# A fourth raw weight buffer in the mixers of a two-layer hybrid decoder, paid for with single copies of the rotary step's small tiles

## Chip, core and metric

The kernel runs on one core of a Trainium2 chip. The metric is the device time of one launch in microseconds (us); lower is better. A core has five engines with queues of their own: TensorE (PE, with its weight loads shown as PEld), VectorE (DVE), ScalarE (ACT), GpSimd (POOL) and SyncE (SP), which here only issues DMAs.

## The reference

Two layers over 512 tokens of width 1024, all in float32. A layer is a mixer and an MLP:

```python
def hybrid_layer(x, ...):
    h = rmsnorm(x, norm_mix)
    z = h @ w_in                       # 1024 -> 4360 columns
    q_a, k_a, v_a, q_m, k_m, v_m, o_m, if_m, gates = jnp.split(z, splits, axis=-1)
    q_a = partial_rope(rmsnorm(q_a, att_q_norm), cos, sin)   # 8 heads of 64, first 16 dims turned
    k_a = partial_rope(rmsnorm(k_a, att_k_norm), cos, sin)   # 2 heads of 64
    att = sliding_window_attention(q_a, k_a, v_a, sinks)     # window 128, blocks of 128
    hm = mlstm_chunkwise(q_m, k_m, v_m, i_pre, f_pre)        # 4 heads, exact, running-max stabiliser
    hm = rmsnorm(hm, m_head_norm) * sigmoid(o_m)
    mixed = sigmoid(g_a) * (att @ w_att_branch) + sigmoid(g_m) * (hm @ w_m_branch)
    x = x + mixed @ w_out
    u = relu(rmsnorm(x, norm_ffn) @ w_ff1)                   # 1024 -> 4096
    return x + (u * u) @ w_ff2
```

## The kernel before

*Matrix products.* Each float32 operand is split into a rounded high part (`h`) and the rest (`l`), both of type float32r, and a product is three matmuls: high by high, high by low, low by high (`mm3`). For a weight chunk of 128 x 512 this is what happens in the mixer, in `chunk`: SP loads it into a tile of the pool `wraw` (L161 or L166); ACT copies it to `wh` (L186); DVE subtracts and gives `wl` (L187); both lie in the pool `wsp`, four buffers each. Then PE runs the chunk's matmuls: 4 slices of 128 by 3. A tile of `wraw` is free again when its `wl` is made, a pair of `wsp` when PE has read it.

*A mixer* runs, in this order, the projections q and k,v,i,f by tokens (`tok_steps`), mLSTM's q,k and the branch gates by features (`feat_steps`), the value and output-gate columns as seven products instead of eight (`vo_steps`; their loads are L813 and, with added halves, POOL's L817), the two attention projections (`a_steps`, from `w_att_branch`), the mLSTM projection (`m_step`, from `w_m_branch`, loads L1098 into `wraw` too, split by L196 and L197) and `w_out` (`p_step`, again seven products; loads L1111, L1120). `weave` lays between the steps of these products the side work: rope, attention (8 units of a block and a key head in each layer), the gates, the mLSTM.

*Order.* No order is written out by hand for whole engines. A planner goes through the instructions by priority and simulates the engines by a cost model; `tc.high_priority` pulls an instruction ahead, `tc.issue_after` puts it behind another on its engine. The planner also knows which buffer is free when, so the number of buffers of a pool enters into the order of every engine. DMAs of SP are issued in the order of SP's queue: one that waits for its buffer holds those behind it.

*Rope* (`rope`) scales the heads on DVE (L591) and then, on POOL, makes t1 = x cos (L594), t2 = the swapped halves times sin (L595, L597), and writes the sum back (L599). It runs for each of 4 blocks on the 2 key heads and the 8 query heads. t1 and t2 come from the pool `small`, tags `rp2`, `rq2` (128 bytes a partition) and `rp8`, `rq8` (512 bytes), three buffers each as all tags of that pool have.

*Room.* SBUF tiles of a partition, one after the other: constants, `small`, `inp` (the normed activations), and from there the phase's own pools. Mixer and MLP take turns in that last room (mixer 0, MLP 0, mixer 1, MLP 1), so a tile of one phase waits for the tiles of the phase before that lie under it (`reuse_waits="tile"`). In units of 2,048 bytes from the start of that room, worked out from the pools' sizes in their order:

| units before | mixer pool | units after the change |
|---|---|---|
| 0-3 | `wraw` | 0-4 |
| 3-11 | `wsp` (4 wh, 4 wl) | 4-12 |
| 11-34 | `act` (23 slots) | 12-35 |
| 34-42 | `prods` | 35-43 |
| 42-60 | `tmp` (18 slots) | 43-61 |
| from 60 | `mid`: `kvi`, `sel`, `cm2`, then `mid10`, `mid6` | from 61 |

| units, before and after | MLP pool |
|---|---|
| 0-14 | `uraw`: seven tiles of 4,096 bytes |
| 14-26 | `comb` |
| 26-34 | `uspl` (uh, ul) |
| 34-50 | `spl`: 4 wh (34-42), 4 wl (42-50), 128 x 1024 each |
| 50-60 | raw weights 9, 8, 7, 10, 3 |
| 60-64 | raw weights 0, 1 |
| 64-70 | raw weights 4, 5, 6 |
| 70-72 | raw weight 2 |

*The MLP* loads its raw weights (512 KB each) by SP at L1299 in the order 0, 1, 2, 9, 8, 7, 10, 3, 4, 5, 6, each issued behind the one before; adds further blocks to them by POOL (L1425, L1674); splits them by `two_parts` (L1263 on ACT, L1264 on DVE).

Of the kernel before, what the change touches and what calls it, by code (L numbers as in the profile page):

```python
# [16 lines left out]
P = 128  # L17
# [9 lines left out]
ROPE = 16  # L27
# [6 lines left out]
def hybrid_kernel(ctx, tc, x, norm_mix, w_in, att_q_norm, att_k_norm, att_sinks, m_gate_bias,  # L34
# [27 lines left out]
    def nm(s):  # L62
        uid[0] += 1
        return f"{s}_{uid[0]}"
# [4 lines left out]
    def pool(phase, name, bufs):  # L69
        now[name] = phase.enter_context(tc.tile_pool(name=name, bufs=bufs, reuse_waits="tile"))  # L70
        return now[name]
# [29 lines left out]
    def sm(shape, tag, bufs=None):  # L101
        return small.tile(list(shape), F32, tag=tag, name=nm(tag), bufs=bufs)
# [340 lines left out]
    def mixer(l, norm, late, order, phase):  # L443

        W = w_in[l]
        pool(phase, "wraw", 3)
        pool(phase, "wsp", 4)
        pool(phase, "act", 23)
        prods = pool(phase, "prods", 1)
# [137 lines left out]
        def rope(xv, b, nh):  # L587

            r0 = 0 if nh == HQ else 8
            ct, st = tabs[nh != HQ]  # L590
            ve.tensor_tensor(xv, xv, rqk[:, b, r0:r0 + nh].unsqueeze(2).to_broadcast([P, nh, HD]), op=ALU.mult)  # L591
            t1 = sm([P, nh, ROPE], f"rp{nh}")
            t2 = sm([P, nh, ROPE], f"rq{nh}")
            gp.tensor_tensor(t1, xv[:, :, 0:ROPE], ct[:, l, b:b + 1, :].to_broadcast([P, nh, ROPE]), op=ALU.mult)  # L594
            gp.tensor_tensor(t2[:, :, 0:8], xv[:, :, 8:16],  # L595
                             st[:, l, b:b + 1, 0:8].to_broadcast([P, nh, 8]), op=ALU.mult)
            gp.tensor_tensor(t2[:, :, 8:16], xv[:, :, 0:8],  # L597
                             st[:, l, b:b + 1, 8:16].to_broadcast([P, nh, 8]), op=ALU.mult)
            gp.tensor_tensor(xv[:, :, 0:ROPE], t1, t2, op=ALU.add)  # L599
# [9 lines left out]
        def k_vec(b):  # L609
            rope(kvi[:, b, 0:128].rearrange("p (h d) -> p h d", d=HD), b, HKV)  # L610
# [36 lines left out]
        def q_vec(b):  # L647
            rope(q_tok[b].rearrange("p (h d) -> p h d", d=HD), b, HQ)
# [1185 lines left out]
    for l in range(DEPTH):  # L1834
        with start if l == 0 else ExitStack() as phase:
            if l > 0:
                psum_pools(phase, 3)
            norm = mixer(l, norm, late, order, phase)
        with ExitStack() as phase:
            psum_pools(phase, 2)  # L1840
            norm = mlp(l, norm, phase)
        late = []
        if norm:
            late = [(0.5 + 0.5 * k, lambda k=k, norm=norm: turn_behind(norm, 6 + k)) for k in range(2)]
            late += [(1.25, lambda norm=norm: norm.squares(1))]
            late += norm.steps(0, 1.5, 0.5, lambda k, norm=norm: turn_behind(norm, k))
        order = [4, 5, 6, 7, 0, 1, 2, 3]
# [40 lines left out]
```

## Time and profile before

| | us |
|---|---|
| median of 3 runs (lowest, highest) | 1265.22 (1262.96, 1265.27) |
| the profiled execution | 1263.76 |
| its span, first to last instruction | 1262.1 |
| PE busy in it | 1255.6 |
| DVE busy | 1034.8 |
| ACT busy | 813.3 |
| POOL busy | 283.2 |

In the profile a line number is that of the kernel's source. PE's matmuls overlap in the records, since their ends are modelled, so a single one shows longer than the distance to the next. Names are the program's tiles with the buffer numbers left out, `out<-in`. The view of waits lists for each engine who ended its idle time; for SP, which only issues, it lists how long the queue stood. Times inside the profile are counted from the start of the span.

### The profile page before, as it was taken

The numbers are of one execution on the slowest core, as the hardware profiler recorded it, in microseconds if no ns is written. First come the engines' busy times: TensorE is split into PE (matmuls) and PEld (weight loads), VectorE is DVE, ScalarE is ACT, GpSimd is POOL, SyncE is SP. The second block draws the span as 40 slices with busy tenths as digits, with TensorE's granted clock in tenths as the row PEclk, the third lists the DMA queues.
The fourth block names the chain that finished last, engine by engine and source line by source line (L and its number), as shares of the span: only waits on it lengthen the run. The fifth ranks groups of instructions, "written<-read, shape, count | busy, mean of one in ns | idle before, by whom it ended". The sixth has DMA issues, their size and how long they took to land.

```text
span 1262.1 us, 19896 instructions
## 1 busy us (share of the span) xinstructions
PE 1255.6 (99%) x7170; PEld 1098.8 (87%) x7170; DVE 1034.8 (82%) x1645; ACT 813.3 (64%) x1442; POOL 283.2 (22%) x373
## 2 busy tenths in 40 slices
PE   9999999999999999999999999999999999999998
PEld 7888888888999899999888888888889999999987
DVE  5788988688998877878857989876889978778787
ACT  5578578645785665656554885876467766556563
POOL 4514131021122021031115042310303211311300
PEclk9999999999999999999999999999999999999999
DMA  5424573468899889997224354634779988998953
GB/s 159 114 69 134 127 130 93 142 137 212 179 250 182 233 170 211 235 187 190 36 75 118 89 137 110 117 111 132 156 208 189 240 191 228 171 223 207 201 134 100
DMA packets 145538, 199.68 MB, mean 158 GB/s; under 512 B 11032, under 2 KB 85632, under 8 KB 145440
## 3 DMA queue, kind: packets, MB, share of 16 engines
q0 software_dynamic: 50432, 68.30, 33.9%
q1 hardware_dynamic: 94016, 129.72, 33.5%
q8 instruction: 56, 0.92, 0.3%
q10 hardware_dynamic: 992, 0.40, 0.1%
q14 instruction: 42, 0.34, 0.1%
HBM read 195.24 MB, written 2.10 MB: 156 GB/s over the span
## 4 chain that ended last, share of the span: by engine, by line
PE 99%; DMA 0%; ACTq 0%; DVE 0%; issue 0%; DVEq 0%
PE mm L47 84%; PE aux L47 13%; PE aux L52 3%; DMA grow<-in_norm_mix_dram 0%; ACTq L373 0%; ACTq L380 0%; DVE x L1327 0%; DVEq L1884 0%
## 5 line engine op out<-in xcount | busy, mean ns | idle before, releaser
L1263 ACT ACTIVATE wh<-raw 128x1024 fp32r<-128x1024 f32 x224 | 235.0, 1055 | 149.9 <-PE mm L47 75.9
L1264 DVE TENSOR_TENSOR wl<-raw,wh 128x1024 fp32r<-128x1024 f32 x224 | 271.3, 1221 | 73.5 <-ACT wh L1263 70.7
L47 PE MATMUL mm<-i,wh 128*128 128x256 f32 (+1 forms) x1344 | 331.1, 339 | 0.0
L47 PEld LDWEIGHTS mm<-i,wh 128*128 128x128 f32 x1344 | 223.8, 190 | 19.4
L47 PE MATMUL mm<-i,wl 128*128 128x256 f32 (+1 forms) x672 | 224.7, 335 | 0.0
L47 PE MATMUL mm<-wh,uh 128*128 128x512 f32 x440 | 172.1, 391 | 0.0
L47 PE MATMUL mm<-wl,uh 128*128 128x512 f32 x440 | 171.7, 390 | 0.0
L47 PE MATMUL mm<-wh,ul 128*128 128x512 f32 x440 | 171.3, 389 | 0.0
L1425 POOL DMA_DIRECT2D raw<-in_w_ff_dram x56 | 72.5, 1375 | 349.3 <-DVE wl L1264 85.4
L47 PEld LDWEIGHTS mm<-i,wl 128*128 128x128 f32 x672 | 127.4, 190 | 13.5
L186 ACT ACTIVATE wh<-w 128x512 fp32r<-128x512 f32 (+1 forms) x143 | 85.3, 603 | 60.9 <-PE mm L47 44.0
L187 DVE TENSOR_TENSOR wl<-w,wh 128x512 fp32r<-128x512 f32 (+1 forms) x143 | 95.5, 671 | 34.8 <-ACT wh L186 34.0
L47 PE MATMUL mm<-t,wh 128*128 128x256 f32 x576 | 104.5, 283 | 0.0
L47 PE MATMUL mm<-wh,i 128*128 128x512 f32 (+1 forms) x352 | 99.5, 357 | 0.0
L47 PEld LDWEIGHTS mm<-wh,ul 128*128 128x128 f32 x440 | 82.6, 188 | 17.5
L47 PEld LDWEIGHTS mm<-wh,uh 128*128 128x128 f32 x440 | 82.8, 188 | 16.2
L47 PEld LDWEIGHTS mm<-wl,uh 128*128 128x128 f32 x440 | 82.8, 188 | 15.5
L47 PEld LDWEIGHTS mm<-t,wh 128*128 128x128 f32 x576 | 90.7, 192 | 1.3
L1674 POOL DMA_DIRECT2D raw<-in_w_ff_dram x40 | 48.4, 1214 | 169.8 <-DVE wl L1264 120.7
L47 PE MATMUL mm<-t,wl 128*128 128x256 f32 x288 | 81.5, 283 | 0.0
L1327 DVE SCALAR_TENSOR_TENSOR x<-mm,ms,x 128x512 f32<-128x512 f32 x102 | 72.4, 745 | 10.7 <-PE mm L47 10.4
L47 PEld LDWEIGHTS mm<-wh,i 128*128 128x128 f32 x352 | 62.0, 188 | 8.6
(336 smaller groups left out, 2536.6 us busy)
## 6 DMA issues: line engine op xcount, KB each, us to landing
raw<-in_w_ff_dram SPq DMA_DIRECT2D x144, 512.0 KB, 6.0
raw<-in_w_ff_dram POOLq DMA_DIRECT2D x96, 512.0 KB, 7.8
w<-in_w_in_dram SPq DMA_DIRECT2D x112, 256.0 KB, 2.8
a<-in_w_in_dram POOLq DMA_DIRECT2D x32, 256.0 KB, 5.7
qa<-in_w_out_dram POOLq DMA_DIRECT2D x12, 512.0 KB, 6.0
a<-in_w_in_dram SPq DMA_DIRECT2D x16, 256.0 KB, 4.4
w<-in_w_att_branch_dram SPq DMA_DIRECT2D x16, 256.0 KB, 3.1
w<-in_w_m_branch_dram SPq DMA_DIRECT2D x16, 256.0 KB, 2.7
```

The costliest lines, as they stand in the source:

```text
L47: latest[0] = nc.tensor.matmul(*args, **kw)
L52: latest[0] = nc.tensor.transpose(*args)
L186: sc.activation(wh[:, :off], raw[:, :off], AF.Copy)
L187: ve.tensor_tensor(wl[:, :off], raw[:, :off], f32(wh[:, :off]), op=ALU.subtract)
L1263: last_high[0] = sc.activation(hi, src, AF.Copy)
L1264: last_rest[0] = ve.tensor_tensor(lo, src, f32(hi), op=ALU.subtract)
L1327: ve.scalar_tensor_tensor(xh[:, cc], ps[i][:, cc], ms[j][:, b:b + 1], xh[:, cc], op0=ALU.mult, op1=ALU.add)
L1425: return gp.dma_start(to[h], src(h, i, j), accum_op=ALU.add)
L1674: gp.dma_start(to[h], src(h, i, j), accum_op=ALU.add)
```

## The change

The pool `wraw` gets four buffers in both mixers. The rope's t1 and t2 get one buffer for each tag instead of three. This frees 2 x 2 x (512 + 128) = 2,560 bytes a partition below the phase pools and takes 2,048 bytes more inside the mixers' room; the tables above show what that does to the places.

```diff
     def mixer(l, norm, late, order, phase):
 
         W = w_in[l]
-        pool(phase, "wraw", 3)
+        pool(phase, "wraw", 4)
         pool(phase, "wsp", 4)
         pool(phase, "act", 23)
...
             ve.tensor_tensor(xv, xv, rqk[:, b, r0:r0 + nh].unsqueeze(2).to_broadcast([P, nh, HD]), op=ALU.mult)
-            t1 = sm([P, nh, ROPE], f"rp{nh}")
-            t2 = sm([P, nh, ROPE], f"rq{nh}")
+            t1 = sm([P, nh, ROPE], f"rp{nh}", 1)
+            t2 = sm([P, nh, ROPE], f"rq{nh}", 1)
             gp.tensor_tensor(t1, xv[:, :, 0:ROPE], ct[:, l, b:b + 1, :].to_broadcast([P, nh, ROPE]), op=ALU.mult)
```

## The prediction

> **What bounds the kernel now.** I read the page first: busy shares, the chain that ended last, then the waits of TensorE.
>
> ```profile
> span 1262.1 us, 19896 instructions
> PE 1255.6 (99%) x7170; PEld 1098.8 (87%) x7170; DVE 1034.8 (82%) x1645; ACT 813.3 (64%) x1442; POOL 283.2 (22%) x373
> PE 99%; DMA 0%; ACTq 0%; DVE 0%; issue 0%; DVEq 0%
> ```
>
> PE works 1255.6 of 1262.1 us, and the chain back from the end is PE from one end to the other. So 6.5 us is all the time in which PE visibly does nothing. Next, the view of waits for PE alone, and the busy time by stretch (stretch, its length, then busy us and instruction count of PE, PEld, DVE, ACT, POOL, the granted clock, DMA share and GB/s). The first mixer ends at about 316, the second lies between about 628 and 942.
>
> ```profile
> PE aux L47 <- POOL ones L114: 1.2, 1, 1.2
> PE aux L52 <- DMA grow<-in_norm_mix_dram: 0.8, 1, 0.8
> 0.00:28.00 28.00, 25.96 (x124) 20.94 (x124) 12.77 (x22) 16.20 (x34) 15.25 (x37) 1.00 0.62 175
> 28.00:130.00 102.00, 101.85 (x545) 86.35 (x546) 86.69 (x213) 72.58 (x202) 36.92 (x70) 1.00 0.41 106
> 130.00:200.00 70.00, 70.00 (x333) 57.92 (x333) 65.74 (x134) 49.32 (x103) 18.94 (x26) 1.00 0.54 115
> 380.00:628.00 248.00, 248.00 (x1517) 223.52 (x1516) 202.25 (x199) 152.02 (x166) 47.83 (x41) 1.00 0.82 183
> 700.00:800.00 100.00, 99.89 (x494) 82.55 (x493) 91.74 (x202) 73.93 (x192) 26.15 (x41) 1.00 0.48 120
> 1005.00:1262.00 257.00, 252.87 (x1537) 227.22 (x1535) 205.58 (x204) 150.36 (x163) 45.46 (x37) 1.00 0.81 182
> ```
>
> The idle 6.5 us is placed: 2.04 at the start (two waits of 1.2 and 0.8, for a memset and for the gains), 4.13 behind the last matmul, and 0.15 + 0.11 = 0.26 in the two attention stretches. No wait of PE for a weight is listed at all. The clock is 1.00 throughout. Whatever helps the weights of the mixers can win 0.26 us of visible idle time.
>
> **The change part by part.**
>
> *The fourth raw buffer.* What it takes away are waits of SP for a buffer, and waits of ACT for a transfer. The waits of SP in 20 to 254 us, then in 640 to 880 (total, times, longest):
>
> ```profile
> SPq L166 <- DVE wl L187: 93.8, 36, 11.0
> SPq L166 <- DVE wl L187: 95.7, 41, 11.0
> ```
>
> The load of a chunk is issued as soon as the chunk three before it has been split (`wl`). With four it follows the chunk four before, so it is issued one chunk earlier. The waits of ACT, in 28 to 254 and then in 628 to 880:
>
> ```profile
> ACT wh L186 <- PE mm L47: 18.3, 15, 2.6
> ACT t L196 <- DMA w<-in_w_m_branch_dram: 3.5, 3, 1.8
> ACT wh L186 <- DMA w<-in_w_in_dram: 3.4, 4, 1.4
> ACT wh L186 <- DMA w<-in_w_att_branch_dram: 2.6, 3, 1.3
> ACT wh L186 <- PE mm L47: 25.8, 21, 2.6
> ACT t L196 <- DMA w<-in_w_m_branch_dram: 3.8, 3, 2.4
> ACT wh L186 <- DMA w<-in_w_in_dram: 3.8, 4, 1.7
> ACT wh L186 <- DMA w<-in_w_att_branch_dram: 2.2, 2, 1.3
> ```
>
> The transfers hold ACT for 3.5 + 3.4 + 2.6 = 9.5 us in the first mixer and 3.8 + 3.8 + 2.2 = 9.8 in the second; about 19 us of ACT's waiting can go. ACT then waits for the next thing, which the same rows show: a `wh` buffer that PE's matmuls free (18.3 and 25.8 us, four `wsp` buffers, unchanged). And nothing of it reaches PE. One chunk that waited for its transfer, the fourth of the second mixer:
>
> ```profile
> 629.72 2.19 SPq L166 DMA_DIRECT2D w<-in_w_in_dram  x3
> 632.29 0.63 ACT L186 ACTIVATE wh<-w 128x512 fp32r<-128x512 f32 x1 [0.84 <-DMA w<-in_w_in_dram]
> 632.96 0.69 DVE L187 TENSOR_TENSOR wl<-w,wh 128x512 fp32r<-128x512 f32 x1
> 644.04 0.48 PE L47 MATMUL mm<-wh,i 128*128 128x512 f32 x1
> ```
>
> Its `wl` is done at 632.96 + 0.69 = 633.65; PE gets to it at 644.04, after three chunks of 12 matmuls with the transposes of the norm between. So 10.4 us of cover lie over the 0.84 us that would go. Tighter is the first mixer around 40 us, where PE takes the 264-wide chunks faster; but the stretch 28 to 130 has 0.15 us of idle PE in all. Gain: between 0 and 0.26 us; I take 0.1.
>
> What it may cost. SP's queue is in order: a load issued earlier lets the loads behind it (L813, L1098, L1120) go earlier as well. In the first 28 us an earlier weight could take bandwidth from the x loads: 256 KB at the 175 GB/s of the first stretch is 1.5 us. But those loads stand ahead of it by `issue_after`, and after its two waits PE isn't idle there; I take 0, with 1.5 as the far end.
>
> *One copy of the rope's small tiles.* The instructions are the same; only the reuse distance shrinks. The rope's last POOL instruction on the q half (min/median/max ns):
>
> ```profile
> L599 POOL TENSOR_TENSOR a<-rp,rq x8: 453/482/791, 56.7 to 690.3; 128x128 f32<-128x128 f32 x8
> ```
>
> Both tiles are written (L594 to L597) and read (L599) by POOL alone, in its own order, and in POOL's timeline every L599 stands ahead of the next L594 of the same width already. So the single copy asks for no order that isn't there. Were it not so, a rope would wait for one L599, at most 0.79 us, on an engine that is 22% busy. I take 0; the far end is one such wait per layer that shows at PE, 2 x 0.79 = 1.6 us.
>
> *What lies over what.* 2 KB more for `wraw`, 2.5 KB less below it: seen from the mlp, whose pools use the same room, every mixer pool behind `wraw` moves up one 2 KB slot (units counted from the phase pools' start, in the tables of the section on the kernel). Waits for reused room change at the mixer's end. Two moves count.
>
> First, the mlp's raw 0 (units 60 to 62) lay over `kvi` and now lies over the last `tmp` slot and `kvi`. SP's issues at this place, SP's waits by what ended them, and a raw transfer's landing time:
>
> ```profile
> 276.17 35.24 SPq L1299 DMA_DIRECT2D raw<-in_w_ff_dram  x11
> SPq L1299 <- DMA x<-st: 34.5, 3, 17.5
> SPq L1299 <- DVE i L197: 16.9, 2, 8.6
> DMA to landing us min/median/max: 3.6/6.8/16.9
> ```
>
> Raw 0 is issued at 276.17; then SP stands 17.5 us for a stage tile (to 294) and 8.6 us for a split that reads a `tmp` tile (to 304). At the worst raw 0 also waits to 304, with raws 1 and 2 behind it, which land 6.8 us later, at 311 to 312. They are first read at:
>
> ```profile
> 313.36 1.04 ACT L1263 ACTIVATE wh<-raw 128x1024 fp32r<-128x1024 f32 x1
> 314.44 1.23 DVE L1264 TENSOR_TENSOR wl<-raw,wh 128x1024 fp32r<-128x1024 f32 x1 [2.17 <-ACT wh L1263]
> 310.37 0.48 PE L47 MATMUL mm<-wh,a 128*128 128x512 f32 x1
> 315.71 0.39 PE L47 MATMUL mm<-wh,a 128*128 128x512 f32 x1
> 316.62 0.49 PE L47 MATMUL mm<-i,wh 128*128 128x256 f32 x2
> 316.94 0.29 PE L47 MATMUL mm<-i,wl 128*128 128x256 f32 x1
> ```
>
> So 20 us of delay are hidden, with 1 to 2 us to spare in the worst case. Cost 0.
>
> Second, the first `wh` of the mlp (units 34 to 36) lay over `prods` and now has half of it over the last `act` slot. Four of those slots hold the operands of the mixer's last product, whose 24 matmuls PE runs from 310.37 to 315.71 + 0.39 = 316.1. The product goes by token halves of its operands, so two of the four come free halfway, at about 313.2, and two at 316.1; all others are free before. `wl` is ready at 314.44 + 1.23 = 315.67, and PE wants it at 316.94: 1.27 us of cover. If the slot is free before 313.36 + 1.27 = 314.6, nothing is lost; if only at 316.1, 316.1 - 314.6 = 1.5 us in each layer. Of 23 slots two are bad, and the planner can take another `wh` buffer first; I take 0, with 3 us as the far end.
>
> *Sum.* 1263.76 us of the profiled execution (1262.1 of span and 1.7 around it) - 0.1 = 1263.7. The three runs have their median 1.5 us above the profiled one, at 1265.22; so 1265.1 for a median.
>
> *A rule against the 99%.* The row above has PEld at 57.92 of 70 us (83%) in 130 to 200, and at 223.52 of 248 (90%) in the mlp. The Trainium skill, Perfetto Trace Analysis, section Identifying the Most-Contended Engine, says that the busy share of matmuls is a bad measure, since they are pipelined, and that the busy share of weight loads is a better one. By that rule the mixers have hidden gaps; by the busy row they have 0.26 us. The spacing of matmuls decides between them; pieces of the chain with start, us and count:
>
> ```profile
> 135.86 13.83 PE mm L47 x60
> 150.12 13.63 PE mm L47 x60
> 254.20 51.88 PE mm L47 x228
> ```
>
> 512-wide matmuls follow each other every 230.5, 227.2 and 227.5 ns. The lower share in the mixers comes from longer matmuls, not from gaps; at most 0.2 us in 13.83 is hidden.
>
> **The rivals.**
>
> *Faster, hidden gaps.* If those 0.2 us in 13.83 were late weights everywhere, the two mixers (630 us) would hide 9 us. For it: 230.5 against 227.2. Against it: no wait of PE in the list, and cover of 10 us over the chunk shown. Taken at a third: 1262. Chance 0.06.
>
> *Slower, the mlp's first `wh`.* The mechanism above: its room is free only when PE leaves the mixer's last product. It decides from 314.6 on, and costs up to 1.5 us twice: 1268. For it: 1.27 us of cover is the least that I found; against it, the planner's choice among four `wh` buffers. Chance 0.09.
>
> *Slower, another order.* The planner orders ACT and DVE by its own clock; with raw weights there earlier it can put one more split ahead of a link of the softmax or mLSTM chain. The low half of a split:
>
> ```profile
> L187 DVE TENSOR_TENSOR wl<-w,wh x143: 421/685/978, 7.7 to 875.7; 128x512 fp32r<-128x512 f32 x127, 128x264 fp32r<-128x264 f32 x16
> ```
>
> One split more ahead is 0.69 us on DVE, which is at 92% in 700 to 800; if each of the 16 attention units of both layers paid it to PE, 11 us; a third of them, 4 us: 1269. Chance 0.08.
>
> *The change does nothing*, since SP stands at other waits anyway: the same time as the forecast, and counted with it.
>
> **How the numbers follow.** The runs span 1262.96 to 1265.27, 2.3 us or 0.18%; 0.2% (2.5 us) is about what a measurement here can tell from no change. No change in time: 0.77, at 1265.1, own range 1263 to 1266.5. Faster rival 0.06, slower ones 0.17 at 1268 and 1269. Faster by over 0.2% needs less than 1262.7: 0.06. Slower needs more than 1267.7: about 0.15 of the slower cases' 0.17. Same: 0.79. The range reaches from the low end of the runs to 1268.5, where the first slower case is held and the second begins.
>
> **What would show it.** Right: SP's wait for `wl` L187 shorter, ACT's 19 us of waits for w transfers nearly gone and its waits for PE longer, PE idle 6.5 us as before, raw 0 of the mlp issued near 296 to 304 and not at 276. Wrong: a wait of PE listed in the mixers or at 316 and 942, PE's matmuls in the mixers further apart than 227 to 231 ns, or the second mixer's start or end moved against the first matmul by over 1 us.

## The result: 0.6% slower, and the profile after

| | before | changed |
|---|---|---|
| median of 6 runs each, us | 1263.49 | 1271.66 |
| lowest to highest, us | 1262.96 to 1265.27 | 1268.9 to 1273.08 |
| the profiled execution, us | 1263.76 | 1268.90 |
| its span, us | 1262.1 | 1267.2 |

The ratio of changed to before is 1.0058 (95% interval 1.0043 to 1.0072). A second set of runs gave 1.0050 (1.0038 to 1.0063). A ratio is estimated from all runs of both kernels and is not the quotient of the two medians. Two runs below, 5970.37 us in e_force and 1294.61 us in e_rope1, lie far above the others of their kernel and are counted in no ratio or median.

The mean of the six runs is 7.3 us above that before. The profiled execution is the fastest of the six, and its span is 5.1 us longer; these 5.1 us are what the views below account for. The other five left no trace; three of them, at 1272.23 to 1273.08, have a mean clock of 0.998 or 0.999.

The page of the changed kernel: its span, busy times and the chain that ended last.

```profile
span 1267.2 us, 19899 instructions
PE 1256.4 (99%) x7170; PEld 1098.9 (87%) x7170; DVE 1034.0 (82%) x1645; ACT 813.7 (64%) x1442; POOL 282.7 (22%) x373
PE 97%; DMA 1%; DVE 1%; ACT 1%; issue 0%; SPq 0%; ACTq 0%; DVEq 0%
```

The work is the same; the chain is no longer PE from end to end, and PE is idle for 1267.2 - 1256.4 = 10.8 us where it was 6.5. PE's waits in the changed kernel (total, times, longest):

```profile
PE mm L47 <- DVE wl L1264: 3.0, 2, 1.5
PE aux L47 <- POOL ones L114: 1.2, 1, 1.2
PE mm L47 <- ACT i L199: 0.8, 2, 0.4
PE aux L52 <- DMA grow<-in_norm_mix_dram: 0.6, 1, 0.6
PE mm L47 <- DVE i L200: 0.6, 2, 0.3
```

Three waits are new, each twice, that is once in each layer: 3.0 + 0.8 + 0.6 = 4.4 us. Two are the same as before, at the start of the kernel. The stretches say where the new ones are: 30 us around the start of the first mlp and 34 us around that of the second, before and then changed (columns as in the prediction).

```profile
310.00:340.00 30.00, 30.00 (x230) 28.71 (x229) 26.56 (x32) 23.84 (x36) 3.80 (x4) 1.00 0.80 209
936.00:970.00 34.00, 34.00 (x249) 32.10 (x248) 30.37 (x35) 26.33 (x39) 6.25 (x5) 1.00 0.78 191
```

```profile
310.00:340.00 30.00, 27.71 (x205) 25.87 (x204) 23.99 (x29) 21.74 (x34) 2.58 (x2) 1.00 0.68 176
936.00:970.00 34.00, 31.71 (x233) 29.54 (x232) 28.01 (x33) 24.58 (x38) 3.37 (x3) 1.00 0.71 188
```

PE loses 2.29 us in each. Counted by the starts of its matmuls, whose ends are only modelled, it is 3.0 us in each: the distance of each start from the one before, less the median distance for the width of that one, summed over 300 to 340 is 3.4 us against 0.4 before, and over 940 to 980 it is 3.3 against 0.3. That is 6.0 us in all, of which the start of the kernel gave back some 0.4 in this execution and the rest of the span some 0.5, in pieces below 0.3: 5.1 = 1267.2 - 1262.1.

Where PE waits, the timeline of the changed kernel's PE shows, rows with a wait in brackets:

```profile
316.32 0.60 PE L47 MATMUL mm<-i,wh 128*128 128x256 f32 x3
318.40 0.39 PE L47 MATMUL mm<-i,wl 128*128 128x256 f32 x1 [1.48 <-DVE wl L1264]
...
333.24 0.50 PE L47 MATMUL mm<-i,wh 128*128 128x256 f32 x2 [0.40 <-ACT i L199]
334.02 0.39 PE L47 MATMUL mm<-i,wh 128*128 128x256 f32 x1 [0.28 <-DVE i L200]
```

The mlp's first matmul by a low half stands 1.48 us for `wl`. Why that is late is seen in DVE's timeline, before (the row of the first `wl`, at 314.44, stands in the prediction) and changed:

```profile
315.58 1.28 DVE L1187 TENSOR_TENSOR x<-x,mm 128x512 f32<-128x512 f32 x2
316.78 1.22 DVE L1309 TENSOR_TENSOR x<-i,i 128x1024 f32<-128x1024 f32 x1
317.91 2.35 DVE L1264 TENSOR_TENSOR wl<-raw,wh 128x1024 fp32r<-128x1024 f32 x2
```

```profile
314.02 0.69 DVE L1187 TENSOR_TENSOR x<-x,mm 128x512 f32<-128x512 f32 x1 [2.50 <-PE mm L47]
315.38 0.69 DVE L1187 TENSOR_TENSOR x<-x,mm 128x512 f32<-128x512 f32 x1 [0.68 <-PE mm L47]
315.99 1.22 DVE L1309 TENSOR_TENSOR x<-i,i 128x1024 f32<-128x1024 f32 x1
317.12 3.49 DVE L1264 TENSOR_TENSOR wl<-raw,wh 128x1024 fp32r<-128x1024 f32 x3
```

Before: first `wl`, two additions onto x (L1187), the sum x22 (L1309, which adds the high and low part of one block of the mlp's input), more `wl`. After: the two additions, the sum, and only then the first `wl`, at 317.12 instead of 314.44. No bracket stands at 317.12: DVE does not wait for room there. It had stood 2.50 and 0.68 us for PE at the two additions, which were planned ahead of `wl`. ACT's timeline says the same of the high half. Its first `wh` is issued at 313.36 in both kernels, in the changed one directly behind four squares of the norm where before there were three:

```profile
312.73 0.63 ACT L293 ACTIVATE junk<-x 128x512 bf16<-128x512 f32 x1
313.27 0.18 ACT L293 ACTIVATION_READ_ACCUMULATOR junk<-x 128x1 f32 x1
313.36 2.94 ACT L1263 ACTIVATE wh<-raw 128x1024 fp32r<-128x1024 f32 x3
```

So the reading after the result was: the first `wh` lies over the last `act` slot (by the program's addresses it starts where that slot starts); PE reads the slot's tile last in the twelfth of the 24 matmuls of the mixer's last product, the first of the two in the row below, so to 312.6:

```profile
312.24 0.62 PE L47 MATMUL mm<-wh,a 128*128 128x512 f32 x2
```

On the chip nothing has to wait for it. But the planner, by its own clock, would see that room free later, and give ACT and DVE another order, and PE with them. The planner's own times are not on record; that they are the link is inferred from the changed order and from the missing wait.

### The profile page after: what moved, and what is told of

The parts are those of the page before. It is cut to its first block, busy times and chain, and to the rows that moved or that the text cites. A ratio compares the mean times of both kernels' runs of the same rounds, so it can differ in the third digit from the quotient of the medians.

```text
span 1267.2 us, 19899 instructions
## 1 busy us (share of the span) xinstructions
PE 1256.4 (99%) x7170; PEld 1098.9 (87%) x7170; DVE 1034.0 (82%) x1645; ACT 813.7 (64%) x1442; POOL 282.7 (22%) x373
## 4 chain that ended last, share of the span: by engine, by line
PE 97%; DMA 1%; DVE 1%; ACT 1%; issue 0%; SPq 0%; ACTq 0%; DVEq 0%
PE mm L47 82%; PE aux L47 12%; PE aux L52 2%; DMA raw<-in_w_ff_dram 1%; DMA grow<-in_norm_mix_dram 0%; DVE i L200 0%; ACT i L199 0%; DVE wl L1264 0%; ACT wh L1263 0%; ACT u L1537 0%; DVE wl L197 0%; SPq L1299 0%; DVE x L1309 0%; ACT x L1360 0%; ACTq L380 0%
## 5 line engine op out<-in xcount | busy, mean ns | idle before, releaser
L187 DVE TENSOR_TENSOR wl<-w,wh 128x512 fp32r<-128x512 f32 (+1 forms) x143 | 94.8, 668 | 30.6 <-ACT wh L186 29.4
```

What stands on the lines that cost most here:

```text
L187: ve.tensor_tensor(wl[:, :off], raw[:, :off], f32(wh[:, :off]), op=ALU.subtract)
```

## The experiments

Three theories went into the first four runs. A: the first `wh` over the `act` slot. B: the mixers' order, changed by the fourth buffer. C: the mlp's raw 0 over a `tmp` slot and its late issue. The kernels are the changed one with these lines added or replaced.

**e_shift**: three buffers as before, but the same shift of the rooms.

```diff
-        pool(phase, "wraw", 4)
+        pool(phase, "wraw", 3)
+        pool(phase, "pad", 1).tile([P, T], F32, tag="pad", name=nm("pad"))
```

> Three raw weight buffers as before, the rope's tiles once, and 2 KB left empty behind wraw in the mixer, so that all other pools lie as in the changed kernel: the new places without the fourth buffer. Theory A (the mlp's first wh tile now lies over an act slot that PE reads to the end of the mixer, so the mlp starts late): as the changed kernel, 1269 to 1273 us, with PE waiting for wl L1264 some 1.6 us at 318 and at 946. Theory B (the fourth buffer changes the order inside the mixers): as before, 1263 to 1264. Theory C (raw 0 of the mlp is issued 20 us later and its transfers are late): 1269 to 1273.

Measured: 1270.77 us, ratio to before 1.0051 (1.0039 to 1.0064). The loss without the fourth buffer: B falls.

**e_padspl**: four buffers, 2 KB of pad ahead of `spl` in the mlp, so that no `spl` tile lies over an `act` slot (the raw weights move too).

```diff
+        pool(phase, "pad", 1).tile([P, T], F32, tag="pad", name=nm("pad"))
         spl = pool(phase, "spl", 4)
```

> The changed kernel with four buffers, and 2 KB left empty in the mlp ahead of the pool spl, so that spl and all raw weights lie over the mixer as before the change; uraw, comb and uspl lie as in the changed kernel. Theory A: as before, 1263 to 1264.5 us, no wait of PE for L1264. Theory B: as the changed kernel, 1269 to 1273. Theory C: 1263 to 1264.5, since the raw weights are back too.

Measured: 1263.48 us, ratio 0.9996 (0.9987 to 1.0005). All its waits of PE:

```profile
PE aux L47 <- POOL ones L114: 1.2, 1, 1.2
PE aux L52 <- DMA grow<-in_norm_mix_dram: 0.9, 1, 0.9
```

**e_padraw**: the same pad behind `spl`, which moves the raw weights and leaves `spl` over the slot.

```diff
         spl = pool(phase, "spl", 4)
+        pool(phase, "pad", 1).tile([P, T], F32, tag="pad", name=nm("pad"))
```

> The changed kernel with the 2 KB left empty behind spl, ahead of the raw weights: only the raw weights lie as before the change, the wh tiles still over the act slot. Theory A: as the changed kernel, 1269 to 1273 us, with PE's 1.6 us waits for L1264. Theory B: the same 1269 to 1273. Theory C: as before, 1263 to 1264.5, raw 0 issued at 276 again.

Measured: 1270.85 us, ratio 1.0048 (1.0036 to 1.0061). Raw 0 is issued early again, and the loss stays, so C falls:

```profile
275.67 35.08 SPq L1300 DMA_DIRECT2D raw<-in_w_ff_dram  x11
```

**e_after2**: the changed kernel again, beside these three.

> The changed kernel again, beside the others on one chip. All theories: 1269 to 1273 us. Its listed waits of PE at the mlps' starts add up to about 5 us, while the runs were up to 9.6 us above before; open is whether runs at a granted clock of 0.998 explain the rest (0.2% of 1270 is 2.5 us). If they do, runs with clock 1.000 lie at 1269 to 1270 and those with 0.998 at 1272 to 1273.

Measured: 1270.88 us, ratio 1.0050 (1.0038 to 1.0063). The question on the clock stays open here: all five runs have a clock of 1.000, and lie from 1269.14 to 1271.13.

So the loss comes and goes with the place of `spl`, and the overlap of the first `wh` is the cause that fits. One other overlap moved with it, and neither these runs nor e_raw3 separate the two: by the tables the first `wl` (units 42 to 44) now lies over the last unit of `prods` as well. The trace of the changed kernel speaks against that one. The last row there that reads a `prods` tile (`p`) ends at 301.62, 11.7 us before the first `wh` starts:

```profile
300.94 0.68 DVE L197 TENSOR_TENSOR a<-p,a 128x512 fp32r<-128x512 f32 x1
```

The next runs ask how the overlap acts.

**e_pad1k**: half the pad, half the overlap.

```diff
+        pool(phase, "pad", 1).tile([P, 2 * P], F32, tag="pad", name=nm("pad"))
         spl = pool(phase, "spl", 4)
```

> The changed kernel with a pad of 1 KB ahead of spl in the mlp, half of what frees the first wh from the act slot: the overlap is 1 KB instead of 2 KB. Theory (a tile waits for all that lies under it, however little, so the cost is there or not): 1270.8 like the changed kernel, wl L1264 again near 317. Rival (cost in proportion to the overlap, or to how far the tiles are moved): 1267 to 1268.

Measured: 1270.86 us, ratio 1.0056 (1.0042 to 1.0071), with the changed kernel's waits of PE (2.9, 0.8 and 0.6 us). Half the overlap costs as much as the whole.

**e_raw3**: no room added; the mlp's raw weight 3 and `spl` change places.

```diff
+        raws_3 = pool(phase, "raws_3", 1)
         spl = pool(phase, "spl", 4)
...
-        for which, tags in (("a", (3, 7, 8, 9, 10)), ("b", (0, 1)), ("c", (4, 5, 6)), ("d", (2,))):
+        for which, tags in (("a", (7, 8, 9, 10)), ("b", (0, 1)), ("c", (4, 5, 6)), ("d", (2,))):
             raws.update(dict.fromkeys(tags, pool(phase, "raws_" + which, 1)))
+        raws[3] = raws_3
```

> The changed kernel with one tile moved: the mlp's raw weight 3, loaded eighth, takes the two units behind uspl, and spl begins two units later, so no spl tile lies over an act slot; everything from unit 60 on stays. No room is added. Theory (only the first wh over the last act slot costs time): as the kernel before, 1263 to 1266, no wait of PE for L1264, PE idle 6.5 us or less. Rival (raw 3 over the act slot now waits and comes late, with the loads behind it, or the pad of the earlier experiment helped by moving the raws): 1268 to 1271.

Measured: 1264.90 us, ratio 0.9999 (0.9990 to 1.0008). PE is idle only at its start. Its raw 0 is issued as late as in the changed kernel, which settles C a second time; the changed kernel's row, then that of e_raw3:

```profile
295.60 14.89 SPq L1299 DMA_DIRECT2D raw<-in_w_ff_dram  x11
297.67 6.71 SPq L1301 DMA_DIRECT2D raw<-in_w_ff_dram  x7
```

**e_order**: e_raw3, so without the overlap, with DVE's order at the mlp's start made by hand that of the changed kernel. The main lines are these, with comments for the reader; `onto_`, `summed` and `wait_sum` only remember the instructions to wait behind.

```diff
...
+            with tc.issue_after(onto_[0].ins):                 # in x22: behind the last L1187
+                plus(scratch["a"], h22, l22)
+            wait_sum[:] = [summed[0]]
...
+            with tc.issue_after(wait_sum.pop().ins) if wait_sum else ExitStack():   # the first wl
+                last_rest[0] = ve.tensor_tensor(lo, src, f32(hi), op=ALU.subtract)
```

> The kernel e_raw3 (no spl tile over an act slot) with DVE's order at the mlp's start made that of the changed kernel: the sum x22 is put behind the mixer's last addition L1187, and the first wl behind that sum. DVE's order is then the changed kernel's, ACT's too but for one square beside the first wh, PE's is the planner's own for it. Theory (the order alone costs the time): the first wl starts near 317 and PE waits 1.5 us for it in each layer again; 1264.9 + 2 x 1.5 = 1267.9 at the least, 1270.9 with the waits for i near 333. Rival (the overlap in the room is needed, the order is only its sign): 1263 to 1266 as e_raw3, PE not idle at 316 and 942.

Measured: 1270.68 us, ratio 1.0047 (1.0032 to 1.0061). The timeline, ACT's first `wh` and DVE's rows:

```profile
312.73 1.04 ACT L1267 ACTIVATE wh<-raw 128x1024 fp32r<-128x1024 f32 x1
316.09 1.22 DVE L1315 TENSOR_TENSOR x<-i,i 128x1024 f32<-128x1024 f32 x1
317.22 3.49 DVE L1269 TENSOR_TENSOR wl<-raw,wh 128x1024 fp32r<-128x1024 f32 x3
```

and PE's waits:

```profile
PE mm L47 <- DVE wl L1269: 3.2, 2, 1.6
PE mm L47 <- ACT i L199: 0.8, 2, 0.4
PE mm L47 <- DVE i L200: 0.6, 2, 0.3
```

`wh` is ready at 313.77, 3.45 us before DVE takes it up. The room is free, the order is late, and all three waits are back. Without the overlap, DVE's order at this place is enough to make the loss; the order of ACT and PE behind it was left to the planner.

**e_force** (run before e_order): the changed kernel, overlap and all, with x22 put behind the first `wl`.

```diff
+            with tc.issue_after(last_rest[0].ins):
                 plus(scratch["a"], h22, l22)
...
+        prepare(1)
         x22()
```

> The changed kernel with its room as it is; the mlp's first weight is split ahead of the sum x22 in the program, and x22 is put behind that split's low half on DVE, so DVE runs the first wl (L1264) before the two additions L1187 and the sum L1309. Theory (the order in which DVE issues costs the time, not the chip waiting for the room): the first wl starts near 314.4 to 315 instead of 317.1 and PE's two waits of 1.5 us for it go; 1270.9 - 3.3 = 1267.6 if PE's waits for i (L199, L200) near 333 stay, 1264.5 if they go too. Rival (the room itself holds wh or wl until PE has left the mixer's last product): wl still starts after 315.2 and the time stays above 1269.5.

Measured: 1269.39 us, the median of four runs from 1268.44 to 1271.02, ratio 1.0042 (1.0028 to 1.0056). The theory's 1267.6 or less was not reached. Of the rival's two signs `wl` after 315.2 came true, and the time is too close to its bound of 1269.5 to tell. DVE's timeline, then PE's waits:

```profile
315.66 0.69 DVE L1187 TENSOR_TENSOR x<-x,mm 128x512 f32<-128x512 f32 x1 [0.68 <-PE mm L47]
316.27 1.22 DVE L1264 TENSOR_TENSOR wl<-raw,wh 128x1024 fp32r<-128x1024 f32 x1
317.40 1.22 DVE L1309 TENSOR_TENSOR x<-i,i 128x1024 f32<-128x1024 f32 x1
```

```profile
PE mm L47 <- ACT i L199: 2.1, 2, 1.1
PE mm L47 <- DVE wl L1264: 0.9, 2, 0.5
```

It is not the rival's reason, though: no wait stands at `wl`, and what DVE waits for is PE's last product, at the addition ahead of it. I had thought of L1309 alone. The edit moves `wl` ahead of it, but not ahead of the two additions; `wl` starts at 316.27, not at 314.4 to 315. So this run does not decide between theory and rival by its time; e_order does. PE's wait for it falls from 3.0 to 0.9 us, and the planner's order behind it lets the wait for `i` grow from 0.8 to 2.1. With the overlap in place, one dependency set by hand brings the three waits from 4.4 us to 2.1 + 0.9 + 0.6 = 3.6; in the time the two kernels do not come apart.

**e_rope1**: the kernel before with the single rope copies alone.

```diff
-        pool(phase, "wraw", 4)
+        pool(phase, "wraw", 3)
```

> The kernel before with the rope's t1 and t2 kept once, and three raw buffers: the mixer's and the mlp's rooms both begin 2.5 KB lower and stand to each other as before. The prediction's step (single copies cost 0, at most 1.6 us): 1263 to 1266, as the kernel before. Rival (POOL waits for L599, and attention for POOL): 1266 to 1267, with waits of PE in the stretches 28 to 130 and 700 to 800 above 0.3 us.

Measured: 1263.84 us (median of ten), ratio 1.0002 (0.9993 to 1.0011), no new wait of PE.

**e_warm**: e_raw3 with two more matmuls at the kernel's start, an attempt at a version faster than both.

```diff
             x0 = norm.transposes(0)
+        with tc.issue_after(latest[0].ins):
+            for _ in range(2):
+                pe.matmul(idle[:, :2 * P], ones, ones.unsqueeze(1).to_broadcast([P, 2, P]), start=True, stop=True)
```

> The kernel e_raw3 with two more 256-wide matmuls of ones behind the first transposes of x, in the time in which PE waits for the gains (4.5 to 5.6 us). In some profiles PE's matmuls turn from 420 to 230 ns (512 wide) near 4.2 us, in others only near 9.9 us, and the span is 2 us longer; the runs of each kernel fall into two groups 2 us apart. Theory (PE's idle time there delays the turn): the runs gather at 1263.0 to 1263.8, median about 1263.3. Rival (the turn isn't tied to what PE does there): two groups again, near 1263.2 and 1265.2, and up to 0.9 us on both, since in the slow start the added matmuls reach past 5.6 us.

Measured: 1263.45 us, 1262.98 to 1264.21 in 11 runs, where the kernel before had 1263.14 to 1265.95 in 14; ratio 0.9994 (0.9985 to 1.0003). The longer of the two groups is gone: none of 11 runs is above 1264.5, where the kernel before has 6 of 14, and e_raw3, on which this builds, had 6 of 11 in its own set. The interval of the ratio holds 1, so a faster version is not shown.

## Why the prediction was wrong

*The step that failed* is the second of what lies over what: "Of 23 slots two are bad, and the planner can take another `wh` buffer first; I take 0, with 3 us as the far end." The planner took exactly that buffer. Then the price was looked for in the wrong place. I asked when the chip finds the slot free ("If the slot is free before 313.36 + 1.27 = 314.6, nothing is lost"). It was, at 312.6, and the time was lost all the same. The room enters the planner's order, most likely through its own clock, whose times are not the trace's, and comes out as another order of three engines; DVE's alone brought the loss back with the room free (e_order, 1.0047). The place was named and got a chance of 0.09; the mechanism and the size were not: 3.0 us in each layer by matmul starts instead of at most 1.5, since the changed order has more than one late operand (`wl` at 318, `i` at 333 and 334).

*Held*, point by point. The fourth buffer's gain is hidden: e_raw3 and e_padspl have it and are level with before (0.9999 and 0.9996). ACT's waits for w transfers, 9.5 and 9.8 us before, in the same two stretches of the changed kernel are 4.0 and 1.7, and those for PE grew from 18.3 and 25.8:

```profile
ACT wh L186 <- DMA w<-in_w_in_dram: 2.7, 2, 2.0
ACT t L196 <- DMA w<-in_w_m_branch_dram: 1.3, 1, 1.3
ACT t L196 <- DMA w<-in_w_m_branch_dram: 1.7, 1, 1.7
ACT wh L186 <- PE mm L47: 19.9, 16, 2.6
ACT wh L186 <- PE mm L47: 28.0, 22, 2.6
```

The rope copies cost nothing that shows (e_rope1). Raw 0 was issued at 295.60, where 296 to 304 was forecast, and the late issue cost nothing that shows (e_raw3). The other two rivals, hidden gaps in the mixers and another order inside them, did not come: e_shift carries the whole loss with three buffers, and PE is no more idle in the mixers than before.

*One sign did not come.* SP's waits for `wl` L187 were to be shorter, as what the fourth buffer takes away. In the same two stretches, where they were 93.8 and 95.7 us, they are:

```profile
SPq L166 <- DVE wl L187: 87.3, 33, 11.0
SPq L166 <- DVE wl L187: 100.7, 40, 10.9
```

The sum is 188.0 us against 189.5. The queue stands for its buffers as long as before, although ACT waits less for what they bring; why was not looked into.

## What to carry to other kernels

When tiles of one phase reuse the room of another and a planner orders the engines, a shift of 2 KB below can change the order, and not only the waits: list which first-used tile comes to lie over a last-used one, and compare the instruction order on each engine, not only the moment at which the chip frees the room. Lay over the last tiles to come free something that is wanted late (raw weight 3 in e_raw3) and not the first operand of the next phase. And a cover of 1.27 us read from one order is no cover if the edit can change that order.

## What the runs showed that was not expected

*PE's clock was once halved for a while behind a short idle.* In the profile of e_pad1k the 1.5 us wait ends at 318.68. From 319.5 on, 256-wide matmuls come every 213 ns instead of 120, for 3.3 us; its stretches give the granted clock (third figure from the end):

```profile
316.00:320.00 4.00, 2.40 (x17) 1.95 (x16) 4.00 (x5) 3.54 (x6) 0.00 (x0) 0.93 0.09 32
320.00:324.00 4.00, 4.00 (x25) 4.00 (x25) 3.83 (x4) 1.05 (x1) 0.00 (x0) 0.64 0.57 167
324.00:328.00 4.00, 4.00 (x36) 4.00 (x35) 2.93 (x3) 2.04 (x4) 1.30 (x1) 1.00 0.97 304
```

The middle one has 25 matmuls, the next 36; by the starts the slow stretch costs some 1.6 us on top of the wait itself. The same wait at 948 in the same execution has no such stretch, nor has either in the first profile of the changed kernel. So the wait as its cause is a guess from one case. Runs of the kernels with the wait that are above 1272 have a mean clock of 0.998 or 0.999, but so have some between 1270 and 1271.2 (e_shift, e_padraw). The Trainium skill, TensorE: Matmul & The Clock Gate, section Part 1: The HAM clock gate, says that the clock halves after at least one idle window of some 3.4 us, on a window that runs free of the kernel. The slow stretch is about as long as that window; but it came behind a wait of 1.5 us, and no run here has an idle of 3.4 us in mid-kernel to set beside it.

*The start of the kernel has two lengths.* PE begins slowly; in e_padspl's profile the slow time ends during the x transposes at 3.94, in e_after2's it lasts to 9.9, as the same four `wh` matmuls show (1.18 against 2.05 us), with the clock printed as 1.00 in both:

```profile
5.59 0.23 PE L52 MATMUL aux<-ident,grow 16*128 16x16 f32 x1 [0.93 <-DMA grow<-in_norm_mix_dram]
6.44 1.18 PE L47 MATMUL mm<-wh,i 128*128 128x512 f32 x4
```

```profile
5.45 0.28 PE L52 MATMUL aux<-ident,grow 16*128 16x16 f32 x1 [0.45 <-DMA grow<-in_norm_mix_dram]
6.96 2.05 PE L47 MATMUL mm<-wh,i 128*128 128x512 f32 x4
```

In three of the twelve profiles the slow time lasts beyond 9 us (e_after2, e_shift, e_raw3), and all three executions are in the longer group of their kernel. This fits the 2 us between the two groups into which the runs of most kernels fall (for the kernel before, beside e_warm: eight from 1263.14 to 1263.91, six from 1264.6 to 1265.95). With e_warm, which fills PE's wait for the gains, all 11 runs are in the lower group. Whether the idle time decides it, or the added matmuls in another way, was not tried.
